# Attention that multiplies V with the weights of four query tiles at a time, in one kernel for a two-mixer encoder layer

## The chip, the core and the metric

The kernel runs on one core of one Trainium2 chip. The metric is the device time of one execution in microseconds (us), as the median of several runs.

The core's engines appear under these names: PE (TensorE, matrix products; PEld is its loading of the stationary operand), DVE (VectorE), ACT (ScalarE), POOL (GpSimd) and SP (which issues most DMAs). Each works through its own list of instructions in order and waits at an instruction until what it needs is there.

## The reference

One layer of an encoder with two attention mixers, A and B, for 1024 new positions of one stream and 32 further positions of another that has a cache of 512. Everything is float32. Cut to what matters here:

```python
# mixer A: top-256 keys by an indexer, softmax over those that are left
logits = einsum('bqhd,bqkhd->bqhk', q, kg) * HEAD_DIM ** -0.5     # masked
p = softmax(logits);  o_a = einsum('bqhk,bqkhd->bqhd', p, vg)

# mixer B: stick breaking, strictly causal
z = einsum('bqhd,blhd->bhql', q, k) * HEAD_DIM ** -0.5
sp = where(causal, softplus(z), 0);  tail = cumsum(sp, reverse=True) - sp
a = where(causal, exp(log_sigmoid(z) - tail), 0);  o_b = einsum('bhql,blhd->bqhd', a, v)

m = sigmoid(gate_a) * (o_a @ w_branch_a) + sigmoid(gate_b) * (o_b @ w_branch_b)
h = x + m @ w_out
y = h + square(relu(rmsnorm(h) @ w_up)) @ w_down
```

Each mixer has 8 heads of 64 channels. What changes is the product of the weights (p, or a) with V for the 1024 positions.

## The kernel before

Every product is made from float32 numbers that are split into a high and a low part, since PE multiplies the parts at full speed: V stands as 64 columns of high parts beside 64 of low ones, and the weights are split after they are transposed.

The stages follow each other: projections and the indexer (to about 470 us), attention of mixer B and then of mixer A beside gate and branch projections (about 470 to 905 us), then the merge and the feed-forward part. The attention stage is the one that changes.

*Tiles.* 128 query positions are a tile; a head has eight. For tile t there are L = 128 (t + 1) keys. `weights` (inside `attend`) makes its scores in banks "s" on PE, and `softmax_weights` or `stick_weights` turns them into weights in a place named "p" (128 x 1024, six such places in turn; mixer B also uses four places "rem"). A head is done in two halves (`passes`): half 0 are tiles 0 to 3, half 1 tiles 4 to 7. Mixer B does both halves of a head in a row; mixer A does half 0 of all heads and then half 1 of all heads.

*The product with V.* A half is done in two pairs of tiles, the later pair first. For each two key blocks, up to four 128 x 128 blocks of the weights are transposed into a bank "t" (two banks); `split_pt` copies the bank to a place "tt" as high parts (ACT) and subtracts for the low parts (DVE); there are four places "tt". Then for each key block two matmuls (high, low) with V as the stationary operand add up in 256 columns of the one bank "o". `halves` moves that bank out: ACT copies the low half and DVE adds the high half to it. Only then can the next sum begin in bank "o".

*What sets the order.* The program is recorded first. `Plan` then gives each engine its order: it takes what is ready by its own table of durations, by rank and then by place in the program. Attention has a better rank than the matmuls of gate and branch projections (rank FILL, bank "pj"), which are put where attention isn't ready. Those need weights that were loaded, cast (ACT) and subtracted (POOL or DVE) into five pairs of places "wh", "wl"; the loads of some gates are placed behind an earlier half head (`held`). All instructions are issued in line 440 of `issue`, so rows of the profile are told apart by the names of their tiles: `o<-tt,v` is the product with V, `t<-ident,p` a transpose, `s<-k,q` a score matmul.

Of the kernel before, what the change touches and what calls it, by code (L numbers as in the profile page):

```python
# [10 lines left out]
F32 = mybir.dt.float32  # L11
F32R = mybir.dt.float32r
# [11 lines left out]
SEQ = 1024  # L24
# [5 lines left out]
HD = 64  # L30
# [10 lines left out]
LS = PAST + DEC  # L41
# [23 lines left out]
def cut(L):  # L65

    return L // 2 if L in (640, LS) else 512
# [392 lines left out]
class Layer:  # L460
# [787 lines left out]

    def rooms(self, is_a):

        p = self.nc.tile(self.att, [128, SEQ], F32, "p", bufs=6)
        return [p] if is_a else [p, self.nc.tile(self.att, [128, SEQ], F32, "rem", bufs=4)]

    def attend(self, h, is_a, passes=(0, 1)):

        nc, at = self.nc, self.att
        g = h if is_a else H + h
        direct = is_a and passes[0] == 1 and h >= H - 2
        if direct and h == H - 2:
            self.last = nc.tile(at, [128, SEQ], F32, "last", tag="v", bufs=3)  # L1260
        kk = nc.tile(at, [128, SEQ], F32R, "k", bufs=3)
        v = nc.tile(at, [128, 8, 128], F32R, "v", bufs=3)
        dk = self.dk[g].rearrange("s e t -> (s e) t")
        qs = {}
        for i in range(passes[-1] + 1):
            nc.sync.dma_start(kk.bitcast(F32)[:, 512 * i:512 * i + 512], dk[:, 512 * i:512 * i + 512])
            if i in passes:
                qs[i] = nc.tile(at, [128, 2, 512], F32R, "q", bufs=2)
                for s in range(2):
                    nc.sync.dma_start(  # L1270
                        qs[i].bitcast(F32)[HD * s:HD * s + HD],
                        self.dq[g].rearrange("s e t -> e s t")[:, :, 512 * i:512 * i + 512])
            nc.sync.dma_start(v.bitcast(F32)[:, 4 * i:4 * i + 4], self.dv[g, :, 4 * i:4 * i + 4])

        def weights(t, q, *room):
            L = 128 * (t + 1)
            qh, ql = (q[:, s, t % 2 * 128:t % 2 * 128 + 128] for s in range(2))
            parts = []
            for c0 in range(0, L, cut(L)):
                n = min(cut(L), L - c0)  # L1280
                ps = self.bank("s")
                nc.tensor.matmul(ps[:, :n], qh, kk[:, c0:c0 + n], start=True, stop=False)
                nc.tensor.matmul(ps[:, :n], ql, kk[:, c0:c0 + n], start=False, stop=True)
                parts.append((c0, ps[:, :n]))
            if is_a:
                return self.softmax_weights(parts, L, self.mask[t], self.fq[:, t, h:h + 1], room[0])
            return self.stick_weights(parts, L, *room, self.first[:, DEC + SEQ - L:][:, ::-1])

        for i in passes:
            o = nc.tile(at, [64, 512], F32, "o", bufs=2)  # L1290
            for t0 in (4 * i + 2, 4 * i):
                c = 128 * (t0 - 4 * i)
                q = qs[i][:, :, c:c + 256]
                if i:
                    pw = [weights(t, q, *self.rooms(is_a)) for t in (t0, t0 + 1)]
                else:
                    room = self.rooms(is_a)
                    pw = [weights(t0 + j, q, *(z[:, 512 * j:512 * j + 512] for z in room)) for j in range(2)]
                po = self.bank("o")[:, :256]
                for j0 in range(0, t0 + 2, 2):  # L1300
                    pt = self.bank("t")
                    blocks = [(j, u) for j in (j0, j0 + 1) for u in range(2) if j <= t0 + u]
                    for m, (j, u) in enumerate(blocks):
                        nc.tensor.transpose(
                            pt[:, m * 128:m * 128 + 128], pw[u][:, j * 128:j * 128 + 128], self.ident)
                    parts = self.split_pt(pt, 128, 128 * len(blocks))
                    for j in (j0, j0 + 1):
                        lo = 128 if j > t0 else 0
                        s0 = 256 * (j - j0)
                        for z in range(2):  # L1310
                            nc.tensor.matmul(
                                po[:, lo:256], v[:, j], parts[:, z, s0:s0 + 256 - lo],
                                start=j + z == 0, stop=j + z == t0 + 2)
                self.halves(po, o[:, c:c + 256], self.last[h % 2 * HD:h % 2 * HD + HD, c:c + 256] if direct else None)
            if not direct:
                with nc.rank(FAST):
                    nc.sync.dma_start(self.do[g, :, 512 * i:512 * i + 512], o)
            self.mid = self.mid[1:] + [len(nc.nodes) - 1]

    def attend_new(self, u, is_a):  # L1320

        nc, at, a = self.nc, self.att, self.a
# [10 lines left out]
                    qz[HD * s:HD * s + HD, i, s:s + 7:6], self.dq[g0 + s:g0 + s + 3:2, i, :, new].rearrange("j e t -> e j t"))  # L1333
        for j in range(2):
            kh = nc.tile(at, [128, SEQ], F32R, "kc", tag="k", bufs=3)[:, :LS]
            kl = nc.tile(at, [128, SEQ], F32R, "kl", **(dict(tag="p", bufs=6) if is_a else dict(tag="rem", bufs=4)))[:, :LS]
            k32 = kl.bitcast(F32)[:, :PAST]
            nc.sync.dma_start(k32, self.dc[g0 + 2 * j:g0 + 2 * j + 2].rearrange("j e t -> (j e) t"))
            for i, k in enumerate((kh, kl)):
                for s in range(2):  # L1340
                    nc.sync.dma_start(k.bitcast(F32)[HD * s:HD * s + HD, PAST:], self.dk[g0 + 2 * j + s, i, :, new])
            nc.scalar.copy(kh[:, :PAST], k32)
            nc.gpsimd.tensor_sub(kl[:, :PAST], k32, kh.bitcast(F32)[:, :PAST])
            for i, (q, k) in enumerate(((0, kh), (1, kh), (0, kl))):
                q, first, last = qq[:, q, 128 * j:128 * j + 128], j + i == 0, j + i == 3
                nc.tensor.matmul(ps0[:, :LS // 2], q, k[:, :LS // 2], start=first, stop=last)
                nc.tensor.matmul(ps1[:, :LS // 2], q, k[:, LS // 2:], start=first, stop=last)
        vn = nc.tile(at, [128, SEQ], F32R, "vn", tag="k", bufs=3)[:DEC, :512].rearrange("t (j e) -> t j e", j=4)
        nc.sync.dma_start(vn.bitcast(F32), self.dv[g0:g0 + 4, :DEC, NEW].rearrange("j t e -> t j e"))
        parts = [(0, ps0[:, :LS // 2]), (LS // 2, ps1[:, :LS // 2])]  # L1350
        if is_a:
            p = self.softmax_weights(parts, LS, self.mask[8], self.fqs[:, u:u + 1], *self.rooms(is_a))
        else:
            p = self.stick_weights(parts, LS, *self.rooms(is_a), self.first[:, :LS])
        pt = self.bank("t")
# [3 lines left out]
        pt = self.bank("t")  # L1359
        nc.tensor.transpose(pt[:DEC, 0:128], p[:, PAST:LS], self.ident)  # L1360
        now = self.split_pt(pt, DEC, 128)
        po = self.bank("o")[:, :256]
        for j in range(4):
# [6 lines left out]
            for k in range(4):  # L1370
                nc.tensor.matmul(out, vcs[:, k], old[:, :, k * 128 + 32 * j:k * 128 + 32 * j + 32],
                                 start=k == 0, stop=False)
            nc.tensor.matmul(out, vn[:, j], now[:DEC, :, 32 * j:32 * j + 32], start=False, stop=True)
        o = nc.tile(at, [64, 512], F32, "o", bufs=2)
        self.halves(po, o[:, :256])
        s = o[:, :256].rearrange("e (j i t) -> e j i t", i=2, t=DEC)
# [546 lines left out]
```

## Time and profile before

| | |
|---|---|
| median of 3 runs | 1679.69 us (1675.78 to 1680.08) |
| profiled execution | 1679.89 us, its span 1678.1 us |
| PE busy | 1663.3 us, 12244 matmuls and transposes |
| DVE, ACT, POOL busy | 1355.1, 945.1, 804.2 us |
| matmuls `o<-tt,v` of 256 and of 128 columns | 512 and 128 |
| transposes `t<-ident,p` in the attention stage | 596 |
| casts and subtractions into "tt" | 168 each |

A page of the profile gives busy time per engine, the chain of work that ended last, and groups of like instructions with their mean duration. Busy time of PE counts from a matmul's start to its end, and the next one starts before that; how fast PE really goes is seen from start to start. A wait is idle time of an engine and what ended it.

### The profile page before, as it was taken

To read this page: it belongs to the slowest core of one execution; us is meant where nothing else is said; L and a number is where in the kernel's file an instruction comes from. 1 tells how busy PE (TensorE), PEld (TensorE's weight loads), DVE (VectorE), ACT (ScalarE), POOL (GpSimd) and SP (SyncE) were. 2 spreads that over 40 slices of the span, in tenths; PEclk is the share of its full clock that TensorE was granted. 3 is DMA by queue.
4 is the path that set the end of the run, shared out by engine and by line. 5 is a ranking of instruction groups with operands and counts; after the bars stand their busy time and mean duration, and the time that the engine had idled before them with its cause. 6 is when DMAs were issued, how large, how long until landed. Compare 5 with 4: busy or idle time off the path is not lost.

```text
span 1678.1 us, 34748 instructions
## 1 busy us (share of the span) xinstructions
PE 1663.3 (99%) x12244; PEld 1587.8 (95%) x12244; DVE 1355.1 (81%) x2830; ACT 945.1 (56%) x2008; POOL 804.2 (48%) x681
## 2 busy tenths in 40 slices
PE   9999999999999999999999999999999999999999
PEld 9898999899989999998989999999999999999999
DVE  6777899987579889887877649998988997678775
ACT  7556888764366768886665545333333453443431
POOL 4532332344356576354556348544433466345564
PEclk9999999999999999999999999999999999999999
DMA  8243454355573636788764644444444596676674
GB/s 284 61 125 107 142 185 144 99 155 148 163 218 103 181 100 178 190 264 247 227 188 142 178 123 134 157 146 142 142 142 135 198 326 223 204 232 200 222 227 137
DMA packets 182126, 290.31 MB, mean 173 GB/s; under 512 B 29472, under 2 KB 61696, under 8 KB 181920
## 3 DMA queue, kind: packets, MB, share of 16 engines
q1 hardware_dynamic: 181664, 287.91, 55.1%
q8 instruction: 97, 1.59, 0.4%
q14 instruction: 77, 0.63, 0.1%
q10 hardware_dynamic: 288, 0.17, 0.0%
HBM read 195.09 MB, written 94.90 MB: 173 GB/s over the span
## 4 chain that ended last, share of the span: by engine, by line
PE 84%; DVE 7%; DMA 4%; ACT 2%; issue 2%; POOL 1%; SPq 1%; DVEq 0%; ACTq 0%; POOLq 0%
PE pj L440 34%; PE c L440 11%; PE a L440 11%; PE b L440 11%; PE s L440 9%; PE o L440 4%; PE t L440 4%; DVE junk L440 2%; DMA xt<-x 1%; SPq L440 1%; DVE qi L440 0%; DVE y L440 0%; DMA q<-dq 0%; DMA kl<-dc 0%; DVE ta L440 0%
## 5 line engine op out<-in xcount | busy, mean ns | idle before, releaser
L440 PE MATMUL pj<-xl,wh 128*128 128x272 f32 (+2 forms) x1200 | 334.0, 312 | 0.0
L440 POOL TENSOR_TENSOR wl<-wst,wh 128x512 fp32r<-128x512 f32 x125 | 175.4, 1408 | 219.4 <-ACT wh L440 192.9
L440 PE MATMUL pj<-xh,wh 128*128 128x272 f32 (+1 forms) x768 | 251.7, 328 | 0.0
L440 PE MATMUL pj<-xh,wl 128*128 128x272 f32 (+1 forms) x768 | 250.6, 326 | 0.2 <-POOL wl L440 0.2
L440 PEld LDWEIGHTS pj<-xl,wh 128*128 128x128 f32 x1200 | 212.7, 188 | 10.0
L440 ACT CAST wh<-wst 128x512 fp32r<-128x512 f32 x197 | 120.7, 619 | 126.6 <-PE pj L440 35.0
L440 PEld LDWEIGHTS pj<-xh,wl 128*128 128x128 f32 x768 | 144.6, 188 | 10.8 <-POOL wl L440 0.5
L440 PEld LDWEIGHTS pj<-xh,wh 128*128 128x128 f32 x768 | 144.6, 188 | 10.1 <-DVE gz L440 0.3
L440 POOL TENSOR_TENSOR p<-p,rem 128x383 f32<-128x383 f32 (+8 forms) x66 | 107.2, 1639 | 64.7 <-DVE rem L440 31.1
L440 ACT CAST wh<-us 128x512 fp32r<-128x512 f32 x80 | 49.7, 621 | 122.6 <-PE pj L440 34.3
L440 DVE TENSOR_TENSOR tt<-t,tt 128x512 fp32r<-128x512 f32 (+2 forms) x168 | 100.2, 620 | 16.8 <-ACT tt L440 16.0
L440 DVE TENSOR_TENSOR_SCAN rem<-rem,first 128x384 f32<-128x384 f32 (+8 forms) x66 | 107.2, 1642 | 2.0 <-ACT rem L440 1.6
L440 POOL TENSOR_TENSOR wl<-y,wh 128x512 fp32r<-128x512 f32 x46 | 68.6, 1492 | 77.7 <-ACT wh L440 74.7
L440 ACT ACTIVATE junk<-score,cand 128x1024 bf16<-128x1024 f32 (+2 forms) x93 | 96.9, 1042 | 12.5 <-DVE cand L440 11.0
L440 ACT CAST wh<-y 128x512 fp32r<-128x512 f32 x79 | 49.0, 621 | 96.8 <-PE c L440 20.5
L440 ACT CAST tt<-t 128x512 fp32r<-128x512 f32 (+2 forms) x168 | 85.8, 540 | 27.5 <-PE t L440 18.5
L440 PE MATMUL o<-tt,v 128*128 128x256 f32 (+1 forms) x640 | 98.5, 279 | 0.5 <-DVE o L440 0.5
L440 PE MATMUL s<-k,q 128*128 128x512 f32 (+4 forms) x384 | 98.2, 351 | 0.7 <-DMA q<-dq 0.7
L440 PEld LDWEIGHTS o<-tt,v 128*128 128x128 f32 x640 | 90.5, 189 | 6.1 <-DVE o L440 1.1
L440 DVE TENSOR_SCALAR_CACHE_REDUCE junk<-score,cand 128x384 bf16<-128x384 f32 (+1 forms) x124 | 92.9, 749 | 3.1
L440 PE MATMUL t<-ident,p 128*128 128x128 f32 (+1 forms) x596 | 90.7, 275 | 0.0
L440 POOL TENSOR_SCALAR p<-p,nb 128x384 f32<-128x384 f32 (+6 forms) x66 | 53.5, 817 | 70.8 <-DVE nb L440 59.6
(401 smaller groups left out, 5624.3 us busy)
## 6 DMA issues: line engine op xcount, KB each, us to landing
us<-w_down SPq DMA_DIRECT2D x80, 256.0 KB, 3.3
q<-dq SPq DMA_DIRECT2D x64, 256.0 KB, 4.1
du<-us SPq DMA_DIRECT2D x56, 264.0 KB, 2.7
du<-y SPq DMA_DIRECT2D x56, 264.0 KB, 3.0
y<-w_up SPq DMA_DIRECT2D x44, 256.0 KB, 2.8
k<-dk SPq DMA_DIRECT2D x40, 256.0 KB, 4.1
v<-dv SPq DMA_DIRECT2D x40, 256.0 KB, 4.0
xl<-du SPq DMA_DIRECT2D x35, 264.0 KB, 4.7
```

Of the source, the lines that this page charges most:

```text
L440: fn(*args, **kw)
```

## The change

All four tiles of a half have their weights made first. Then one sum with 512 columns fills a whole bank "o". Each key block that all four tiles see has a bank "t" of its own (four transposes, 512 columns); the last two key blocks share one. A matmul covers the columns of all tiles that see the key block: 512, then 384, 256 and 128. The bank is moved out once per half. The places for weights become eight.

```diff
     def rooms(self, is_a):
-        p = self.nc.tile(self.att, [128, SEQ], F32, "p", bufs=6)
+        p = self.nc.tile(self.att, [128, SEQ], F32, "p", bufs=8)
...
-            qh, ql = (q[:, s, t % 2 * 128:t % 2 * 128 + 128] for s in range(2))
+            qh, ql = (q[:, s, t % 4 * 128:t % 4 * 128 + 128] for s in range(2))
...
         for i in passes:
             o = nc.tile(at, [64, 512], F32, "o", bufs=2)
-            for t0 in (4 * i + 2, 4 * i):
-                c = 128 * (t0 - 4 * i)
-                q = qs[i][:, :, c:c + 256]
+            t0, q = 4 * i, qs[i]
+            pw = []
+            for t in range(t0, t0 + 4, 2):
                 if i:
-                    pw = [weights(t, q, *self.rooms(is_a)) for t in (t0, t0 + 1)]
+                    pw += [weights(t + j, q, *self.rooms(is_a)) for j in range(2)]
                 else:
                     room = self.rooms(is_a)
-                    pw = [weights(t0 + j, q, *(z[:, 512 * j:512 * j + 512] for z in room)) for j in range(2)]
-                po = self.bank("o")[:, :256]
-                for j0 in range(0, t0 + 2, 2):
-                    pt = self.bank("t")
-                    blocks = [(j, u) for j in (j0, j0 + 1) for u in range(2) if j <= t0 + u]
-                    for m, (j, u) in enumerate(blocks):
-                        nc.tensor.transpose(
-                            pt[:, m * 128:m * 128 + 128], pw[u][:, j * 128:j * 128 + 128], self.ident)
-                    parts = self.split_pt(pt, 128, 128 * len(blocks))
-                    for j in (j0, j0 + 1):
-                        lo = 128 if j > t0 else 0
-                        s0 = 256 * (j - j0)
-                        for z in range(2):
-                            nc.tensor.matmul(
-                                po[:, lo:256], v[:, j], parts[:, z, s0:s0 + 256 - lo],
-                                start=j + z == 0, stop=j + z == t0 + 2)
-                self.halves(po, o[:, c:c + 256], self.last[h % 2 * HD:h % 2 * HD + HD, c:c + 256] if direct else None)
+                    pw += [weights(t + j, q, *(z[:, 512 * j:512 * j + 512] for z in room)) for j in range(2)]
+            po = self.bank("o")
+            for js in [(j,) for j in range(t0 + 2)] + [(t0 + 2, t0 + 3)]:
+                pt = self.bank("t")
+                blocks = [(j, u) for j in js for u in range(4) if j <= t0 + u]
+                for m, (j, u) in enumerate(blocks):
+                    nc.tensor.transpose(
+                        pt[:, m * 128:m * 128 + 128], pw[u][:, j * 128:j * 128 + 128], self.ident)
+                parts = self.split_pt(pt, 128, 128 * len(blocks))
+                s0 = 0
+                for j in js:
+                    lo = max(0, 128 * (j - t0))
+                    for z in range(2):
+                        nc.tensor.matmul(
+                            po[:, lo:], v[:, j], parts[:, z, s0:s0 + 512 - lo],
+                            start=j + z == 0, stop=j + z == t0 + 4)
+                    s0 += 512 - lo
+            self.halves(po, o, self.last[h % 2 * HD:h % 2 * HD + HD, :512] if direct else None)
```

In `attend_new` the place "kl" of mixer A, which shares the places "p", also counts eight.

How the order moves is shown at two places. In an order the number behind a name is that of one tile: t_6855 is one use of a bank "t", the tt with the next number is its split copy, p_6836 one tile's weights. "x4" is four alike in a row.

The first place is PE in mixer B, head 6, second half. Before, the products of its later pair:

```order
L440 MATMUL pj_6733<-xh1_106,wl2_6728 128x272
L440 MATMUL pj_6733<-xh1_106,wh2_6727 128x272
L440 MATMUL pj_6733<-xl1_107,wh2_6727 128x272
L440 MATMUL o_6853<-tt_6855,v_6824 128x256 x4
L440 MATMUL o_6853<-tt_6857,v_6824 128x256 x4
L440 MATMUL o_6853<-tt_6859,v_6824 128x256 x4
L440 MATMUL o_6853<-tt_6861,v_6824 128x256 x2
L440 MATMUL o_6853<-tt_6861,v_6824 128x128 x2
L440 MATMUL t_6871<-ident_91,p_6862 128x128
L440 MATMUL t_6871<-ident_91,p_6866 128x128
```

And with the change:

```order
L440 MATMUL t_6855<-ident_91,p_6832 128x128
L440 MATMUL t_6855<-ident_91,p_6836 128x128
L440 MATMUL o_6848<-tt_6854,v_6812 128x512
L440 MATMUL t_6855<-ident_91,p_6840 128x128
L440 MATMUL t_6855<-ident_91,p_6844 128x128
L440 MATMUL t_6857<-ident_91,p_6832 128x128
L440 MATMUL t_6857<-ident_91,p_6836 128x128
L440 MATMUL t_6857<-ident_91,p_6840 128x128
L440 MATMUL t_6857<-ident_91,p_6844 128x128
L440 MATMUL o_6848<-tt_6856,v_6812 128x512 x2
L440 MATMUL o_6848<-tt_6858,v_6812 128x512
L440 MATMUL t_6859<-ident_91,p_6836 128x128
```

Before, all transposes of the pair lie further up, with projections behind them, and the products come in one piece; now transposes and products alternate, and between the last transpose of t_6855 and the product with tt_6856 stand the four of t_6857.

The second place is PE in mixer A, head 6, second half. Before:

```order
L440 MATMUL pj_7449<-og_7394,wl2_7448 128x512
L440 MATMUL pj_7449<-og_7395,wh2_7447 128x512 x2
L440 MATMUL s_7650<-k_7620,q_7622 128x256
L440 MATMUL o_7589<-tt_7591,v_7576 128x256 x4
L440 MATMUL o_7589<-tt_7593,v_7576 128x256 x4
L440 MATMUL o_7589<-tt_7595,v_7576 128x256 x4
L440 MATMUL o_7589<-tt_7597,v_7576 128x256 x2
L440 MATMUL o_7589<-tt_7597,v_7576 128x128 x2
```

And with the change:

```order
L440 MATMUL t_7576<-ident_91,p_7549 128x128
L440 MATMUL t_7576<-ident_91,p_7554 128x128
L440 MATMUL t_7576<-ident_91,p_7559 128x128
L440 MATMUL t_7576<-ident_91,p_7564 128x128
L440 MATMUL pj_7470<-og_7368,wl4_7469 128x512
L440 MATMUL o_7569<-tt_7575,v_7546 128x512 x2
L440 MATMUL o_7569<-tt_7577,v_7546 128x512
L440 MATMUL t_7578<-ident_91,p_7549 128x128
L440 MATMUL t_7578<-ident_91,p_7554 128x128
L440 MATMUL o_7569<-tt_7577,v_7546 128x512
L440 MATMUL t_7578<-ident_91,p_7559 128x128
L440 MATMUL t_7578<-ident_91,p_7564 128x128
```

Here one projection matmul and the four transposes of t_7576 stand between the last transpose of t_7574 (the row above the first one shown) and the product with tt_7575, where before scores and projections stood ahead of all products of the pair.

More of the change, by code (lines that the diff above doesn't have):

```diff
@@ L1335, in attend_new @@
             kh = nc.tile(at, [128, SEQ], F32R, "kc", tag="k", bufs=3)[:, :LS]
-            kl = nc.tile(at, [128, SEQ], F32R, "kl", **(dict(tag="p", bufs=6) if is_a else dict(tag="rem", bufs=4)))[:, :LS]
+            kl = nc.tile(at, [128, SEQ], F32R, "kl", **(dict(tag="p", bufs=8) if is_a else dict(tag="rem", bufs=4)))[:, :LS]
             k32 = kl.bitcast(F32)[:, :PAST]
```

## The prediction

> **What bounds the kernel now.** I read the page first, then busy time by stretches, then the waits of TensorE, and then single rows of TensorE's timeline for prices.
>
> ```profile
> span 1678.1 us, 34748 instructions
> PE 1663.3 (99%) x12244; PEld 1587.8 (95%) x12244; DVE 1355.1 (81%) x2830; ACT 945.1 (56%) x2008; POOL 804.2 (48%) x681
> PEclk9999999999999999999999999999999999999999
> PE 84%; DVE 7%; DMA 4%; ACT 2%; issue 2%; POOL 1%; SPq 1%; DVEq 0%; ACTq 0%; POOLq 0%
> ```
>
> TensorE (PE) is busy for 99% of the span at full granted clock, and the chain that ended last runs through it for 84%. A second row per engine shows the attention stage (470 to 905 us) apart from what follows.
>
> ```profile
> core 0: us, PE busy (x) PEld busy (x) DVE busy (x) ACT busy (x) POOL busy (x), PEclk, DMA share, GB/s
> 470.00:905.00 435.00, 432.89 (x2991) 400.57 (x2990) 361.55 (x812) 320.93 (x709) 241.19 (x197) 1.00 0.63 186
> ```
>
> In that stage PE is busy 432.9 of 435.0 us; VectorE (DVE) 361.6, which is 83%. PE works on attention where it can and on projections ("pj", the fill) where it can't, so that a late softmax or scan costs nothing as long as fill stands ready. What PE did wait for there is small:
>
> ```profile
> PE s L440 <- DMA q<-dq: 0.7, 1, 0.7
> PE s L440 <- POOL kl L440: 0.6, 1, 0.6
> PE o L440 <- DVE o L440: 0.5, 2, 0.3
> PE pj L440 <- POOL wl L440: 0.2, 1, 0.2
> ```
>
> Together 2.0 us (total, times, longest). So two things decide: what PE's own work becomes, and whether PE gets new waits because its cover moves.
>
> **Prices of PE's work.** A matmul's duration overlaps the next one's, so the price is the distance from start to start. This is a stretch of mixer A's head 6 and the last attention matmuls, in PE's timeline (start, us, name, form of the first, count):
>
> ```profile
> 872.15 2.01 PE L440 MATMUL o<-tt,v 128*128 128x256 f32 x16
> 874.00 1.06 PE L440 MATMUL t<-ident,p 128*128 128x128 f32 x8
> 874.82 0.37 PE L440 MATMUL s<-k,q 128*128 128x256 f32 x1
> 875.02 0.39 PE L440 MATMUL pj<-og,wl 128*128 128x512 f32 x1
> 875.25 0.63 PE L440 MATMUL pj<-og,wh 128*128 128x512 f32 x2
> 875.72 0.40 PE L440 MATMUL pj<-og,wl 128*128 128x512 f32 x1
> 875.95 0.63 PE L440 MATMUL pj<-og,wh 128*128 128x512 f32 x2
> 876.41 0.40 PE L440 MATMUL pj<-og,wl 128*128 128x512 f32 x1
> 876.65 0.63 PE L440 MATMUL pj<-og,wh 128*128 128x512 f32 x2
> 877.12 0.40 PE L440 MATMUL pj<-og,wl 128*128 128x512 f32 x1
> ...
> 895.96 0.46 PE L440 MATMUL o<-tt,v 128*128 128x256 f32 x3
> 896.25 0.68 PE L440 MATMUL pj<-og,wh 128*128 128x512 f32 x2
> ```
>
> From 875.02 to 877.12 stand nine matmuls of 512 columns: 2.10 / 9 = 0.233 us. The sixteen from 872.15 to 874.00 are fourteen of 256 columns and a pair of 128 (the first order piece of head 6 above); the three from 895.96 to 896.25 are one of 256 and a pair of 128. So 14a + b = 1.85 and a + b = 0.29: a = 0.120 us for 256 columns, b = 0.170 us for a pair of 128. From 874.00 to 875.02 are eight transposes and a matmul of 256: (1.02 - 0.12) / 8 = 0.11 us per transpose. For 384 columns the score matmuls serve, by their own durations:
>
> ```profile
> L440 PE MATMUL s<-k,q 128*128 128x512 f32 x160 | 53.7, 410 | 0.7 <-DMA q<-dq 0.7
> L440 PE MATMUL s<-k,q 128*128 128x384 f32 x64 | 17.4, 345 | 0.0
> L440 PE MATMUL s<-k,q 128*128 128x256 f32 x64 | 13.7, 292 | 0.0
> ```
>
> 345 ns lies about midway between 292 and 410, so I take the middle of 0.120 and 0.233, 0.176.
>
> **The change part by part.** *Fewer, wider matmuls with V.* Before there are 512 of 256 columns and 128 of 128; after, 192 of 512, 64 each of 384, 256 and 128. Per head (16 heads) that is 32 x 0.120 + 4 x 0.170 = 4.52 us before, and 12 x 0.233 + 4 x 0.176 + 4 x 0.120 + 2 x 0.170 = 4.32 us after. The saving is 0.20 us per head, 3.2 us in all, although 256 of 640 instructions go: a matmul of 512 costs nearly what two of 256 do (0.233 against 0.240), so most of it comes from the 128 wide ones, which fall by half. Were the 64 of 384 columns as cheap as 256 or as dear as 512, it would be 6.8 or -0.4. As PE is the bound, this saving is on the path.
>
> In the Trainium skill, "TensorE: Matmul & The Clock Gate", section Back-to-back issue gap, an isolated matmul is given N / 2.4 GHz plus about 2.5 ns, which makes two of 256 and one of 512 still more alike; by it the saving would be an estimated 0.7 us and the sum below 1682.5. The trace has 233 ns for 512 columns where that rule has 216, so the rows decide.
>
> *Same work, other place.* Transposes, scores, softmax, scans, splits of a transposed bank (168) and all 1280 rows of SP are as many as before. The eight places for weights add no instruction; PE has no wait for a place of p among its four, so they gain nothing directly. They are what lets four tiles live while the next four are made.
>
> *Evictions.* The sum of a half head leaves its bank once with 512 columns instead of twice with 256.
>
> ```profile
> L440 ACT CAST tt<-t 128x512 fp32r<-128x512 f32 x100 | 57.0, 590 | 17.5 <-PE t L440 11.1 <-PE o L440 3.8
> L440 ACT CAST tt<-t 128x384 fp32r<-128x384 f32 x64 | 30.4, 480 | 10.0 <-PE t L440 7.4 <-PE o L440 1.7
> L440 ACT COPY o<-o 64x256 f32<-64x256 f32 x68 | 25.1, 370 | 39.5 <-PE o L440 38.0 <-DMA wst<-w_bb 0.4
> L440 DVE TENSOR_TENSOR tt<-t,tt 128x512 fp32r<-128x512 f32 x100 | 66.9, 681 | 8.7 <-ACT tt L440 8.1
> L440 DVE TENSOR_TENSOR tt<-t,tt 128x384 fp32r<-128x384 f32 x64 | 34.5, 545 | 8.1 <-ACT tt L440 7.9
> L440 DVE TENSOR_TENSOR o<-o 64x256 f32<-64x256 f32 x64 | 26.1, 407 | 10.1 <-ACT o L440 9.8
> L440 PE MATMUL t<-ident,p x596: 270/272/331, 473.8 to 891.8; 128*128 128x128 f32 x197, 128*32 128x128 f32 x2
> ```
>
> One copy and one add of 512 columns should cost about 0.59 and 0.68 (the rows of that width), against 0.37 and 0.41 for each of two. Nobody but the next chain of products waits for them, since there is one bank "o". PE's wait for them is 0.5 us now; half as many of them, each half a microsecond longer: between -0.5 and +0.5, I take -0.2.
>
> *The cover.* This is the part I weigh most. A product needs its four transposes, their cast on ScalarE (ACT) and the subtraction on DVE: 0.27 + 0.59 + 0.68 = 1.54 us from the last transpose's start, so 1.43 us of other PE work must stand between (for 384 columns 0.27 + 0.48 + 0.55 - 0.11 = 1.19). Before, a pair of tiles has at most four such groups, as many as there are places "tt", so all transposes go ahead and fill stands between them and the products. A half head of four tiles now has up to seven groups, two banks "t" and four places "tt": products and transposes must alternate. I went through all 168 groups in both orders with the prices above. Before, the shortest distance is 1.42 us. After, it falls short at three half heads, where no fill is at hand:
> - Mixer B, head 6, second half: between t_6855 and its product stand four transposes, 0.44 us: short by 1.0. The group behind it waits for DVE, 0.68 against two products of 0.233: 0.2. Together 1.2 us.
> - Mixer A, head 6: four transposes and one fill matmul, 0.68: short by 0.75; the next 0.2; a third (three transposes, two fill) 0.80: short by 0.63. Together 1.6 us.
> - Mixer A, head 7: distances of 1.13 and 0.70: 0.3 and, counting that wait, 0.4. Together 0.7 us.
>
> That is 3.5 us of new waits. The lower end is 0, if fill that the order puts elsewhere has already made PE late; the upper end is all sixteen second halves at 1.4 us, 22 us. I take 3.5, as the rows for cast and subtraction are firm and PE hardly waits anywhere now, so it will arrive there early. A wait is not won back: PE is the bound and its total work is fixed.
>
> **Sum**, against the profiled execution's 1679.9 us (span 1678.1 and 1.8 around it; 0.2 above the median of the runs): 1679.9 - 3.2 - 0.2 + 3.5 = 1680.0 us. The measurement can tell about 0.3%, 5 us, from no change.
>
> **The rivals.** *The cover holds* (17%): the three half heads wait for nothing, because PE gets there late. Then 1679.9 - 3.2 - 0.5 = 1676.2; with the other 1.5 us of waits gone too, 1674.7. For it speaks that DVE and ACT are done early in most groups (DVE sat idle for a cast for 8.1 us over 100 groups); against it the 0.44 us of distance. About half of this chance ends below -0.3%.
>
> *The burst decides* (20%, slower): the products of a half head can't start until its fourth tile's weights are there, then seven groups run through two banks "t". A group holds its bank for 0.44 + 0.16 + 0.59 + 0.68 = 1.87 us, 0.94 with two banks, against 0.44 + 0.47 = 0.91 us of PE's work; so without fill PE loses at the start of every such half head, 1.2 to 1.6 us. Three of sixteen do so by the order; DVE is 83% busy, and where a scan stands ahead of a subtraction more will. From six such half heads on the loss passes 5 us net (6 x 1.4 = 8.4, less 3.4). Eight give 1679.9 - 3.4 + 11.2 = 1687.7; all, 1698.9.
>
> *Weight loads are the bound* (3%): PEld is busy 95%, 1587.8 / 12244 = 0.130 us per load; if loads set PE's pace, 256 fewer give 33 us, 1646.6. Against it: 256 and 512 columns would then take the same 0.13 us or more, and they take 0.120 and 0.233. The Trainium skill, "Perfetto Trace Analysis", section Identifying the Most-Contended Engine, does judge TensorE's headroom by the busy share of weight loads; here the two pitches speak against it.
>
> **How the numbers follow.** My forecast holds 60%, 1680.0 with 1676 to 1684 as its own range, all of it within 0.3%. Of the 17% where the cover holds, 9 end faster and 8 the same; 20% slower; 3% much faster. So faster 0.12, same 0.68, slower 0.20. The range is 1674 to 1688: it leaves out the weight-load case, a few per cent of the first rival and the upper half of the second.
>
> **What would show it.** Right: 384 matmuls o<-tt,v, those of 512 about 0.233 us apart; PE's waits of about 1 us on "DVE tt" in the second halves of head 6 of mixer B and heads 6 and 7 of mixer A, 3 to 4 us in all, which are not among the waits now; PE's work in the stage about 3 us less; the rest of the program unchanged. Wrong: such waits absent (then near 1676), or in most half heads, or 512 columns much above 0.24 us; or new waits for weights of fill ("POOL wl") or for a key load, which I price at no change.

## The result and the profile after

The change makes the kernel slower: 1688.84 us (median of 6 runs, 1687.9 to 1691.4) against 1679.12 of before beside it (6 runs), a ratio of 1.0064 with an interval of 1.0051 to 1.0076. The forecast was 1680.0 with a range to 1688; the time lies just above that range, on the side that had a chance of 0.20. The traces below are of one execution each. That of the changed kernel took 1691.4 us, the longest of its six, so some of its waits may be longer than in a usual one.

These lines of the page of the changed kernel stand against the lines of before with which the prediction begins:

```profile
span 1689.6 us, 34137 instructions
PE 1664.6 (99%) x11988; PEld 1572.1 (93%) x11988; DVE 1356.0 (80%) x2800; ACT 937.8 (56%) x1974; POOL 801.9 (47%) x679
PEclk9999999999999999999999999999999999999999
PE 81%; DVE 7%; DMA 5%; issue 2%; ACT 2%; POOL 1%; SPq 1%; DVEq 0%; ACTq 0%; POOLq 0%
```

PE has 256 fewer matmuls, no less busy time by this count, and a smaller share of the chain (81% for 84%). The attention stage, by the same window as before, 470 to 905 us:

```profile
470.00:905.00 435.00, 423.68 (x2659) 375.37 (x2658) 353.44 (x772) 306.99 (x660) 236.71 (x192) 1.00 0.63 186
```

PE is now idle for 11.3 of the 435.0 us, where it was idle for 2.1. From the first score to the last product with V the stage takes 438.0 us for 427.4; merge and feed-forward are as long as they were, within 1 us. What PE waited for there (total, times, longest):

```profile
PE o L440 <- DVE tt L440: 3.4, 5, 1.8
PE s L440 <- DMA q<-dq: 2.2, 4, 1.0
PE s L440 <- DMA dg<-gz: 1.3, 1, 1.3
PE s L440 <- DVE nb L440: 0.9, 1, 0.9
PE o L440 <- DVE o L440: 0.8, 1, 0.8
PE s L440 <- DVE mx L440: 0.7, 2, 0.4
PE pj L440 <- ACT wh L440: 0.7, 1, 0.7
PE o L440 <- ACT tt L440: 0.5, 2, 0.3
PE o L440 <- POOL vcs L440: 0.4, 1, 0.4
```

Together 10.9 us in place of the 2.0 of the four rows of before. Only 3.9 of them are waits for a split ("DVE tt", "ACT tt"); the rest are loads of q, softmax steps (nb, mx), the eviction, the weights of fill (wh) and one wait in `attend_new` (vcs). Of these the forecast had a term for the eviction alone. Two rows name something else than what the wait was for. The row with dg<-gz stands at the score matmul of 484.50 us; its load of q landed at 484.25, and PE's sequencer went on from the wait at 484.28. The row with nb stands at the score matmul of 737.00 us; there the load landed at 736.86, and the sequencer went on at 736.89. Both are waits for q.

To part PE's own work from such waits, I took for each instruction of PE the distance to the start of the next and subtracted the median distance between neighbours of the same two kinds in both traces. The sum of the medians is PE's own work. What is left over is excess; excess of more than 0.112 us at one place I call a wait. In us:

| attention stage | length | PE's own work | excess | of it waits (places) |
|---|---|---|---|---|
| before | 427.4 | 407.3 | 20.1 | 3.3 (7) |
| changed | 438.0 | 403.5 | 34.5 | 16.3 (27) |
| difference | +10.6 | -3.8 | +14.4 | +13.0 |

The saving is there (forecast: 3.2), and 13.0 us of new waits stand against it (forecast: 3.5). Both depend a little on what counts as one kind (names, shapes or both): over five ways of drawing the kinds, own work falls by 3.7 to 4.7 us and the new waits come to 13.0 to 13.3. Where they stand is seen when the stage is cut into stretches of 90 us; the columns are the length, then busy time and instructions of PE, PEld, DVE, ACT and POOL, granted clock, DMA share and GB/s. Two stretches of before:

```profile
470.00:560.00 90.00, 88.73 (x608) 81.76 (x607) 78.98 (x118) 67.66 (x162) 54.42 (x38) 1.00 0.55 162
...
650.00:740.00 90.00, 90.00 (x650) 84.90 (x649) 77.96 (x229) 77.97 (x175) 43.27 (x48) 1.00 0.74 208
```

The same two of the changed kernel:

```profile
470.00:560.00 90.00, 85.91 (x546) 76.89 (x545) 77.63 (x107) 62.44 (x144) 54.75 (x36) 1.00 0.58 165
...
650.00:740.00 90.00, 84.32 (x531) 73.41 (x530) 70.33 (x197) 69.15 (x154) 46.89 (x46) 1.00 0.66 187
```

PE is busy 2.8 and 5.7 us less there. The second stretch holds the passage from mixer B to mixer A. What it lacks is fill. The work on tiles "pj" alone, 680 to 740 us, of before and then of the changed kernel:

```profile
680.00:740.00 60.00, 36.21 (x184) 26.84 (x184) 3.56 (x7) 0.00 (x0) 1.00 0.83 232
```

```profile
680.00:740.00 60.00, 25.22 (x112) 17.75 (x113) 2.26 (x4) 0.00 (x0) 1.00 0.75 211
```

184 matmuls of fill are down to 112 (PE comes first behind the length). Waiting itself leaves less room for them, so I also counted by the progress of the scores: from one half to five eighths of all score columns, PE does 166 matmuls of fill in the kernel before and 84 in the changed one. The whole stage has as many as it had (1184 for 1182); they now run earlier. Before, a run of fill stands around the first products and scores of the passage; now little does. So PE waits there, first for the eviction of bank "o", then for softmax steps and a split, and at 722.55 us for the weights of fill:

```profile
713.14 0.29 PE L440 MATMUL pj<-xh,wl 128*128 128x272 f32 x1
713.27 0.63 PE L440 MATMUL s<-k,q 128*128 128x512 f32 x2
714.65 1.18 PE L440 MATMUL o<-tt,v 128*128 128x512 f32 x3 [0.75 <-DVE o L440]
...
717.85 0.44 PE L440 MATMUL s<-k,q 128*128 128x384 f32 x1 [0.36 <-DVE mx L440]
```

From 713.5 to 722.6 us the waits come to 4.2 us by start to start.

### The profile page after: what moved, and what is told of

The parts are those of the page before. It is cut to its first block, busy times and chain, and to the rows that moved or that the text cites. A ratio compares the mean times of both kernels' runs of the same rounds, so it can differ in the third digit from the quotient of the medians.

```text
span 1689.6 us, 34137 instructions
## 1 busy us (share of the span) xinstructions
PE 1664.6 (99%) x11988; PEld 1572.1 (93%) x11988; DVE 1356.0 (80%) x2800; ACT 937.8 (56%) x1974; POOL 801.9 (47%) x679
## 4 chain that ended last, share of the span: by engine, by line
PE 81%; DVE 7%; DMA 5%; issue 2%; ACT 2%; POOL 1%; SPq 1%; DVEq 0%; ACTq 0%; POOLq 0%
PE pj L440 33%; PE a L440 11%; PE c L440 11%; PE b L440 10%; PE s L440 8%; PE o L440 4%; PE t L440 4%; DVE junk L440 2%; DMA q<-dq 1%; SPq L440 1%; DMA xt<-x 1%; DMA xl<-du 1%; DVE qi L440 0%; DVE y L440 0%; DMA wst<-w_bb 0%
## 5 line engine op out<-in xcount | busy, mean ns | idle before, releaser
L440 PE MATMUL o<-tt,v 128*128 128x512 f32 (+3 forms) x384 | 102.4, 356 | 4.8 <-DVE tt L440 3.4
L440 POOL TENSOR_SCALAR p<-p,nb 128x128 f32<-128x128 f32 (+6 forms) x66 | 51.6, 786 | 71.6 <-DVE nb L440 55.7
L440 DVE TENSOR_TENSOR wl<-wst,wh 128x512 fp32r<-128x512 f32 x74 | 69.4, 940 | 19.9 <-ACT wh L440 18.8
```

The costliest lines, as they stand in the source:

```text
L440: fn(*args, **kw)
```

## The experiments

Three theories were on record before the first runs. A: eight places for weights let scores run ahead until loads of q bound them. B: transposes and wide products must alternate, because only four groups can be split ahead of the products. C: any new order of the program costs some us, because the tables that place the fill (MIDS, FILL_AHEAD, GATES_BESIDE, FILL_BESIDE) were set for the old one. In the later expectations theory B is also called the alternation or the splits theory and theory C the order theory; the places theory says that each wait of the changed kernel belongs to its place in the program. All ratios are to the kernel before, run beside each. Own work and waits are counted as above, from one trace per run; where only the count of places changes, `attend_new` follows it, which the diffs here don't show.

**Eight places alone** (kernel before):

```diff
-        p = self.nc.tile(self.att, [128, SEQ], F32, "p", bufs=6)
+        p = self.nc.tile(self.att, [128, SEQ], F32, "p", bufs=8)
```

> The kernel before with eight places for weights and nothing else changed. Theory A (eight places let scores run ahead until they wait for their load of q, two places, and SP's loads queue behind it): slower by 2 to 6 us, PE waits for q of over 1.5 us (0.7 before). Theory B (the alternation of transposes and wide products is what costs): no change within 2 us. Theory C (any new order costs, since the tables of fill were set for the old one): slower by 4 to 10 us.

1685.8 us, 1.0037 [1.0024, 1.005]. PE's own work is the same (407.0), its waits are 9.1 us for 3.3, of them 1.6 for a load of q as theory A had it; the others stand at 555, 792 and 880 to 888 us. Two more places, for which PE waited nowhere, cost 7 us, and what they change is the order that the planner makes.

**The changed kernel with six places** (the same edit the other way):

> The changed kernel with six places for weights as before. Theory A: the waits for q go back to under 1 us and 4 to 6 of the 9.7 us come back, about 1683 to 1685. Theory B: no gain, 1688 or more, since the next half head has fewer places to be made in, and waits of products for DVE's subtraction stay above 3 us. Theory C: anything from 1684 to 1692.

1704.76 us, 1.0154 [1.0137, 1.0171]. Own work 404.8, waits 28.2 (21 to 29 by how the kinds are drawn). The wide sums need the eight places; and the waits for q are 4.2 us here too, where theory A had them under 1, so the two added places alone don't make them.

**A third place for q** (changed kernel):

```diff
-                qs[i] = nc.tile(at, [128, 2, 512], F32R, "q", bufs=2)
+                qs[i] = nc.tile(at, [128, 2, 512], F32R, "q", bufs=3)
```

> The changed kernel with three places for q in place of two. Theory A: PE's waits for q (2.2 us, and 1.3 us named after dg<-gz) fall under 1 us, and with SP's queue freer 3 to 6 us come back, about 1683 to 1686. Theory B: at most the 2 to 3 us of those waits, 1686 to 1689. Theory C: anything from 1684 to 1692.

1685.8 us, 1.004 [1.0026, 1.0055], a ratio 0.24% below that of the changed kernel, with intervals that just overlap. The three largest waits of PE in its attention stage:

```profile
PE o L440 <- ACT tt L440: 3.4, 4, 2.5
PE o L440 <- DVE o L440: 3.0, 2, 1.9
PE o L440 <- DVE tt L440: 1.6, 3, 1.2
```

No wait for q is left, but waits of products took their place. Theory A had this time (1683 to 1686) and nearly that of eight places alone. But it has the run with six places against it, and three of those below (five places, five places and other tables, other tables alone), which all came out faster than it said.

**Pairs in ascending order** (kernel before; same work, same places):

```diff
-            for t0 in (4 * i + 2, 4 * i):
+            for t0 in (4 * i, 4 * i + 2):
```

> The kernel before with the earlier pair of tiles first in each half, sums still in pairs: a new order without wide sums. Theory C: slower by 4 to 10 us. Theories A and B: within 2 us of before, so 1677 to 1681; if it is slower by more, part of the loss of the change is the order of its tiles and not the width of its sums.

1686.81 us, 1.0044 [1.0029, 1.0059]. Own work 406.4, waits 10.5. The two largest, 3.9 of them for q:

```profile
PE s L440 <- DMA q<-dq: 3.9, 4, 1.8
PE t L440 <- DVE tt L440: 1.7, 3, 1.1
```

The ascending order, in which the changed kernel also makes its weights, costs by the ratios two thirds of what the whole change does, with no wide product in the program. Theories A and B had it within 2 us of before, theory C 4 to 10 us slower.

**Five places for splits** (changed kernel):

```diff
-        tt = nc.tile(at, [128, 2, 512], F32R, "tt", bufs=4)
+        tt = nc.tile(at, [128, 2, 512], F32R, "tt", bufs=5)
```

> The changed kernel with five places for the splits (tt) instead of four; nothing else. Theory B (transposes and wide products must alternate, because only four groups can be split ahead): one more group goes ahead, so the product waits (o<-DVE tt 3.4, o<-ACT tt 0.5, o<-DVE o 0.8) fall to about 1.5, the loads of q stay at about 4.5; attention stage 434, about 1685. Theory C (any other order of the program costs, since the tables that place the fill were set for the old one): a new order again, so no particular gain; stage 433 to 441, 1684 to 1692, and the big waits stand at other places. Theory A (the loads of q): unchanged, about 1689.

1683.55 us, 1.0027 [1.0018, 1.0036]: 0.37% less than the changed kernel's ratio, and the intervals lie apart. (Its profiled execution, 1678.1, was the shortest of 12, so its trace shows fewer waits than a usual one.)

**One number of the fill tables** (kernel before):

```diff
-MIDS = 1
+MIDS = 0
```

> The kernel before with one number of its fill tables changed (MIDS 0 instead of 1: mixer B's fill may be placed from an earlier mark on); the attention's own instructions are all the same. Theory C: slower by 3 to 7 (1682 to 1686), with TensorE's own work in the stage unchanged at 407 and 3 to 7 us more of waits, for loads of q and for splits. Theories A and B: nothing that they speak of is changed, so 1679 within 2.

1682.73 us, 1.0022 [1.0013, 1.0031]; own work 407.0, waits 7.0. As theory C has it: 3.7 us without a change to attention.

**Five places and other tables** (changed kernel):

```diff
-MIDS = 1
-FILL_AHEAD = 1
+MIDS = 0
+FILL_AHEAD = 2
...
-FILL_BESIDE = (1,1,1,1,2,2,2,2,2,2,2,2,1,2,2,1)
+FILL_BESIDE = (1,0,1,1,1,2,2,2,2,2,2,3,2,2,2,1)
...
-        tt = nc.tile(at, [128, 2, 512], F32R, "tt", bufs=4)
+        tt = nc.tile(at, [128, 2, 512], F32R, "tt", bufs=5)
```

> The changed kernel with five places for splits and other fill tables (MIDS 0, FILL_AHEAD 2, FILL_BESIDE 1,0,1,1,1,2,2,2,2,2,2,3,2,2,2,1). Theory C: with tables that suit the order the waits go back to what before has, and the saving in TensorE's own work (3.8) is left: stage 423 to 426, 1674 to 1678, faster than both kernels. Theory B: only the five places count, so as f1 within 2. Theory A: the waits for q stay, so not below 1684.

1679.26 us, 1.0003 [0.9994, 1.0012]. Level with before, not faster than it as theory C had said, and below what theory B said (as with five places alone, within 2 us): own work 402.4, but waits of 7.2.

**Other tables alone** (changed kernel):

```diff
-MIDS = 1
+MIDS = 0
...
-GATES_BESIDE = (2,1,1,1,1,1,1,0)
+GATES_BESIDE = (1,2,1,1,1,1,1,0)
```

> The changed kernel with four places for splits as it is, and other fill tables alone (MIDS 0, GATES_BESIDE 1,2,1,1,1,1,1,0). Theory C: most of the loss goes, 1679 to 1683, the loads of q wait less (below 2 in place of 4.5). Theory B: the tables don't change the alternation; product waits stay at 4 to 5, 1686 to 1689. Theory A: the waits for q stay, 1687 to 1690.

1684.73 us, 1.0031 [1.0019, 1.0043]: 4 us back, less than theory C said, and the loads of q still wait 3.6 us.

**Wide sums in mixer A alone** (eight places for weights; the pairs as before behind `else`):

```diff
+            if is_a:
                 t0, q = 4 * i, qs[i]
                 pw = []
...
+            else:
+                for t0 in (4 * i + 2, 4 * i):
```

> The changed kernel's sums over four tiles in mixer A alone; mixer B is summed in pairs as before, with eight places for weights. TensorE's own work falls by half of 3.8, 1.9. Places theory (each wait of the changed kernel belongs to its place): mixer B's new waits (q loads at 475, 483 and 688 us, the scan ahead of a subtraction at 520, head 6 at 680; together about 8) go, those at the passage from B to A and in A's heads 6 and 7 stay, about 6: 1679 + 6 - 1.9 = about 1683. Order theory (any new order costs 4 to 8 until the fill tables are set for it): 1681 to 1685, and waits at places that the changed kernel doesn't have, mixer B's included.

1679.56 us, 1.0006 [0.9997, 1.0015]; own work 405.0, 2.3 below before (forecast 1.9), waits 6.1. Better than both theories said. It has 196 matmuls of fill from 680 to 740 us.

**Wide sums in the second halves alone** (the same, by another condition):

```diff
-            if is_a:
+            if i:
```

> Sums over four tiles in the second halves alone (five to seven groups each), in both mixers; first halves in pairs. Own work falls by an estimated 2.1 (16 heads: 3.22 to 3.09 us each by the prices of the prediction). Alternation theory (the loss comes from half heads with more groups than places for splits): all of the product waits stay, so about 1688 to 1690, hardly better than the changed kernel. Order theory: 1681 to 1687, with the waits anywhere.

1682.27 us, 1.0022 [1.0013, 1.0031]; own work 405.0 (2.3 less; forecast 2.1), waits 8.9, of which 1.4 are for splits. Theory B said 1688 to 1690: the loss isn't simply that of the half heads with more than four groups.

**Five places and one other table** (changed kernel):

```diff
-GATES_BESIDE = (2,1,1,1,1,1,1,0)
+GATES_BESIDE = (1,1,2,1,1,1,1,0)
...
-        tt = nc.tile(at, [128, 2, 512], F32R, "tt", bufs=4)
+        tt = nc.tile(at, [128, 2, 512], F32R, "tt", bufs=5)
```

> The changed kernel with five places for splits and one other fill table (GATES_BESIDE 1,1,2,1,1,1,1,0). Order theory: 1676 to 1681, own work 403 and waits near those of before; if the best that tables give is 3.8 less than before, 1675. Splits theory alone: as with five places, 1683.5 within 2.

1676.39 us, 0.999 [0.9981, 0.9999]: faster than both kernels, though by 0.1%. One gate projection moves from beside mixer B's head 0 to beside its head 2. The two stretches that had lost:

```profile
470.00:560.00 90.00, 88.54 (x562) 79.45 (x562) 80.95 (x111) 64.95 (x151) 57.89 (x38) 1.00 0.55 154
...
650.00:740.00 90.00, 89.28 (x590) 81.85 (x589) 73.62 (x223) 74.98 (x161) 45.92 (x50) 1.00 0.72 210
```

PE is 88.5 and 89.3 us busy, nearly the 88.7 and 90.0 of before the change; fill from 680 to 740 us is 166 matmuls, and 159 by the progress of the scores where before has 166 and the changed kernel 84. Own work 403.7, waits 5.0. Theory C had this time (1676 to 1681); theory B alone had 1683.5 within 2 us.

**The same without the wide sums, and without the fifth place.** To see whether that time is owed to the wide sums, the two edits of the last diff were also made one by one: in the kernel before the fifth place, the table, and both; in the changed kernel the table alone.

> The kernel before with five places for splits instead of four. Splits theory (the fifth place helps the changed kernel because its half heads have up to seven groups): a pair has at most four groups, so no gain: 1679 within 2 if the order costs nothing. Order theory: the planner places instructions anew, slower by 2 to 6, 1681 to 1685. If before gains as much as the changed kernel did (5.3), to about 1674, the fifth place isn't about the wide sums.

> The changed kernel with the other table (GATES_BESIDE 1,1,2,1,1,1,1,0) and four places for splits. Order theory: the table does most of it, 1678 to 1682. Splits theory: without the fifth place the table brings no more than the other table did (1684.7), 1684 to 1688.

> The kernel before with the same table (GATES_BESIDE 1,1,2,1,1,1,1,0), nothing else. If the table is simply better, before gains from it too, 1675 to 1677, and the fastest version owes nothing to the wide sums. If a table only suits one order (order theory): 1679 to 1684.

> The kernel before with five places for splits and that table: everything of the fastest version but the wide sums. If the wide sums' own saving of 3.8 reaches the time there, this is 3 to 5 slower than 1676.4, at 1679 to 1682. If the table and the places do it, 1675 to 1677.

| us (ratio to before) | as it was | five places | the table | both |
|---|---|---|---|---|
| sums in pairs | 1679.1 | 1681.58 (1.0021 [1.0012, 1.003]) | 1678.89 (0.9999 [0.999, 1.0008]) | 1679.42 (1.0007 [0.9998, 1.0016]) |
| sums over four tiles | 1688.84 (1.0064 [1.0051, 1.0076]) | 1683.55 (1.0027 [1.0018, 1.0036]) | 1683.65 (1.0028 [1.0017, 1.0038]) | 1676.39 (0.999 [0.9981, 0.9999]) |

The table alone brings the wide sums 5.2 us, the fifth place alone 5.3, and both together 12.4; the pairs gain nothing from either (+2.5 and -0.2) or from both (+0.3). With both, the wide sums are 3.0 us faster than pairs (0.17%; the two intervals touch at 0.9998 to 0.9999), near the 3.8 of own work. So the fastest version does seem to owe its time to them, and the loss of the change seems to have been cover that a fifth place and another place for one gate projection give back. Theory B has the first in it and theory C the second; neither alone was right. The fifth place in pairs cost what theory C said (1681 to 1685), but as worded (any new order costs) it is refuted by the last two runs of pairs, whose order is new and which cost nothing that can be measured. The table alone on the wide sums came out between the two (theory C 1678 to 1682, theory B 1684 to 1688). One thing stays open: the fastest version is the best of seven that were tried with the wide sums in every half, and that no order of the pairs is as fast isn't shown, only that none of the six tried was.

How far fill is the cause can be read across the traces. From 680 to 740 us PE waits 5.0 to 7.6 us in the four with fewer than 140 matmuls of fill there, 0.9 to 4.0 in the six with 140 to 170, and at most 1.8 in the seven with 175 or more. But eight places alone have 195 there, wait nowhere in that stretch and lose their 7 us elsewhere: lost fill at the passage is one way in which an order costs, not the only one.

## Why the prediction was wrong, point by point

*PE's own work: right.* Forecast -3.2 us, measured -3.8 in the changed kernel, and -3.6 in the fastest version; for part of the change -2.3 each (second halves forecast at 2.1). The counting is good to about half a microsecond.

```profile
L440 PE MATMUL o<-tt,v 128*128 128x512 f32 x192 | 66.0, 412 | 2.8 <-DVE tt L440 1.4 <-DVE o L440 0.8 <-ACT tt L440 0.5
L440 PE MATMUL o<-tt,v 128*128 128x384 f32 x64 | 19.0, 349 | 0.0
```

384 matmuls came out as counted; neighbours of 512 columns start 0.232 us apart (median of 73), for the 0.233 that I used, and those of 384 start 0.175 apart, for 0.176.

*Evictions: sizes right, their wait shifted.* A half head's eviction was priced at 0.59 and 0.68 us:

```profile
L440 DVE TENSOR_TENSOR o<-o 64x512 f32<-64x512 f32 x30 | 20.2, 672 | 7.0 <-ACT o L440 6.7
L440 ACT COPY o<-o 64x512 f32<-64x512 f32 x32 | 18.7, 584 | 15.9 <-PE o L440 15.3
```

It took 0.58 and 0.67. PE's wait for it went from 0.5 to 0.8 us, +0.3 where I took -0.2, within the ±0.5: all of it is the one wait at the passage, where no fill stands.

*The cover: the step that failed.* The three half heads that I named do wait, by start to start: mixer B's head 6 for 1.45 us (forecast 1.2), mixer A's head 6 for 1.4 (1.6), its head 7 for 0.6 (0.7), 3.4 us for 3.5. The first of them:

```profile
679.62 0.73 PE L440 MATMUL o<-tt,v 128*128 128x512 f32 x2 [0.25 <-DVE tt L440]
...
681.76 0.50 PE L440 MATMUL o<-tt,v 128*128 128x512 f32 x1 [0.29 <-ACT tt L440]
682.48 0.50 PE L440 MATMUL o<-tt,v 128*128 128x512 f32 x1 [0.22 <-DVE tt L440]
```

But the term, +3.5, was meant for all new waits and held only these: it measured +13.0. I walked through one chain, transposes to split to product, and priced everything else that hangs on the order, "a key load" and weights of fill among them, at no change. Of the 9.6 us missing, about 4.5 are waits of scores for loads of q (at 475, 483, 688 and 736 us), 4.2 the passage without fill, 2.0 one product behind a scan; the other small ones, 2.2, are less than the 3.3 us of before, most of which went (about 1.0, for the load of q at 475, stayed). Of the four loads of q three took 6.9 to 7.6 us from issue to landing, where the median of all 64 is 4.1, and the fourth was issued only 4.4 us before its score. Loads as slow stand in the kernel before too (14 took over 6 us, 10 in the changed one), and PE waited for one of them. SP issues them in order, and its waits for PE's scores, behind which loads queue, rose; that this made the four late isn't shown. Of SP's waits in the stage, before and then changed:

```profile
SPq L440 <- PE s L440: 41.4, 21, 6.6
```

```profile
SPq L440 <- PE s L440: 66.1, 28, 7.1
```

The reason that I gave, that PE "hardly waits anywhere now", was no reason for it to stay so: of the six runs that change only the order of the old sums, none gained, three lost 3.7 to 8.2 us (eight places, ascending pairs, one number), and the others between nothing and 2.5. I had no term for that. The fill that the order "puts elsewhere" was the lower end of my range, as cover; it belonged to the upper end, as cover taken away.

*The rivals.* "The burst decides" had the right side and nearly the time (1687.7), and its remark on a scan ahead of a subtraction is one of the waits. But its mechanism, many half heads that each lose 1.2 to 1.6 us at their first products, isn't what the trace shows: 3.9 of 10.9 us wait for splits, at seven places. That its time comes so near is luck. Even so, the fifth place gave back 5.3 us, more than those waits, since with it the planner also puts fill elsewhere (147 matmuls from 680 to 740 us). How much of the 5.3 is the one and how much the other, the runs don't part. "The cover holds" fell: all three spots waited. "Weight loads are the bound" fell: PEld's busy time went from 1587.8 to 1572.1 us and the time rose. By the Trainium skill, "Perfetto Trace Analysis", section Identifying the Most-Contended Engine, the busy share of weight loads is, beside the share of peak arithmetic, what TensorE's headroom is judged by; here it fell from 95% to 93% while the time rose, with 256 loads fewer and more waits of PE.

## What to carry to other kernels

Where the bounding engine is 99% busy because other work was fitted into its gaps, a reordering needs a term of its own: perturb the order alone (a place more, a loop the other way round) and see what that costs before crediting or blaming the change. Walk through every wait that the order sets, loads and the loss of fill among them, not only the chain that the change touches. A change that saves work but loses time in such a kernel should be tried again with one more buffer in the chain that it lengthens and with the fill placed anew, each also on the old kernel.

## What the runs showed of the hardware

The wait of 2.0 us behind a scan shows how VectorE and GpSimd can hold each other up. Most of VectorE's scans of 256 columns took longer when they began beside GpSimd's arithmetic. Of the changed kernel, VectorE's and GpSimd's timeline and the product that waited:

```profile
518.85 2.41 DVE L440 TENSOR_TENSOR_SCAN rem<-rem,first 128x256 f32<-128x256 f32 x1
518.87 0.06 DVE L440 MEMSET p<- 128x1 f32 x1
521.18 1.12 DVE L440 TENSOR_TENSOR tt<-t,tt 128x384 fp32r<-128x384 f32 x2
...
518.72 3.34 POOL L440 TENSOR_TENSOR p<-p,rem 128x1023 f32<-128x1023 f32 x3 [2.29 <-PE s L440]
...
521.76 0.56 PE L440 MATMUL o<-tt,v 128*128 128x256 f32 x3 [1.80 <-DVE tt L440]
```

A scan of 256 columns takes 0.67 us with nothing beside it. Here it starts 0.13 us after GpSimd's multiply of 1023 columns, which ends at 520.72 us, and ends 0.54 us behind that; the subtraction behind it, and PE's product, wait. Of the sixteen scans of this width in both kernels, thirteen began while GpSimd arithmetic was running. Ten of these end 0.54 to 0.55 us after the operation that they met, with lengths from 0.83 to 2.41 us; one met an operation in its last 0.03 us and lost nothing; in the other two it was the multiply that grew, once to 3.82 us for 1023 columns where the one above took 2.00, while the scan kept its 0.67. The Trainium skill, "SBUF — State Buffer", section Who interferes with whom, says that a VectorE instruction with two inputs in SBUF contends with a GpSimd instruction that reads SBUF, and that the order of issue decides who blocks. Ten of the thirteen agree with that order; in the two where the multiply grew, its start stands 0.20 and 0.47 us ahead of the scan's, so by the starts in the trace they don't. Five of the ten lengthened scans are in the kernel before, and PE waited behind none of them: a reordering can move such a meeting to where a product has to wait, and no count of instructions shows it.
